# A hybrid decoder block on one core: start addresses of matmul operands in SBUF

## The chip, the cores and the metric

The kernel runs on one core of a Trainium2 chip. The metric is the device time of one execution in microseconds (us), as the median of three runs. SBUF is the on-chip memory; each of its 128 partitions holds a row of bytes, and a tile occupies the same bytes in every partition. An address below is the byte at which an operand starts in a partition, and "offset" is that address modulo 512.

## What is computed

One layer of a decoder: a normalization, one wide input projection, two token mixers side by side (gated linear attention, "GLA", and a sparse attention with compressed, selected and window branches, "NSA"), a gated merge with an output projection, and a SwiGLU channel mixer. 512 tokens, width 1024, SwiGLU width 2816, everything in float32.

```python
def reference(x, ...):
    h = rms_norm(x, norm_mix_pre[l])
    proj = h @ w_in[l]
    (...) = jnp.split(proj, split_points, axis=-1)
    o_gla = gla_mixer(g_q, g_k, g_v, g_r, g_a, ...)
    o_nsa = nsa_mixer(n_q, n_kc, n_vc, n_ks, n_vs, n_kw, n_vw, n_gate, ...)
    mixed = (jax.nn.sigmoid(merge_gla) * (o_gla @ w_proj_gla[l])
             + jax.nn.sigmoid(merge_nsa) * (o_nsa @ w_proj_nsa[l]))
    x = x + rms_norm(mixed @ w_out[l], norm_mix_post[l])
    h = rms_norm(x, norm_ffn_pre[l])
    f = (jax.nn.silu(h @ w_ffn_gate[l]) * (h @ w_ffn_up[l])) @ w_ffn_down[l]
    x = x + rms_norm(f, norm_ffn_post[l])
    return x
```

## The kernel before

Activations lie transposed, features on the partitions and tokens along them. A matmul multiplies 128x128 weights (stationary) with a moving operand of 128 rows and 512 tokens ("long") or 256 tokens ("short").

**Three matmuls for one.** Every float32 operand is split into a high part in the format fp32r and the low rest, and each product is three fp32r matmuls: high weights with high activations, high with low, low with high. The weights change with every matmul, so each matmul has a weight load of its own. `prod` (L199–211, matmuls L208 to L210) does this for long products.

**Seven products for eight.** The input projections of pairs of heads, the SwiGLU gate and up projections (but three plain columns) and most of the down projection are done by a scheme of Strassen's kind: two outputs by two halves of the tokens from seven short products, of sums of weights ("a11", "s2", "s3", "s1", "a22", "s4", "a12") with sums of activations ("b11", "t2", "t3", "t1", "t4", "b22", "b21"). A unit is such a set of seven: 7 x 12 = 84 matmuls of 256 tokens in the input units (`in_unit`, matmul L422) and the SwiGLU units (`unit`, matmul L1588), and 7 x 21 = 147 in the down products (`down_product`, L1900, four units, worked through in the order `seq`). Sums and splits of the weights for the next units are made meanwhile: raw weights arrive by DMA, DVE adds (L380 to L383 for the input, `sums_s` and `sums_t` for SwiGLU, `dsum` for down), ACT casts the high part, and the low part is a subtraction on DVE (L393, L1488) or a DMA that adds (L362, L1463).

**Stages in time.** The first normalization and the token-major projections (to 42 us), 12 input units (42 to 164), long input projections with GLA and the compressed branch, the attention among further projections (to about 410), projection and output (`out_half` L1315), plain SwiGLU columns (`ffn_half` L1386), SwiGLU units (`unit`, from 521), the rest of SwiGLU, long down products, the four down units (754 to 826) and the last normalization. Instructions are put in order per engine by the program; a tile's readers and writers wait for each other by semaphores.

**Weight buffers.** Long products take their weights from `Stream`, which fetches a raw tile and splits it into "whi" and "wlo", a pair of tiles with two buffers each. The units use the same two pairs as slots, with "s1", "s2", "s0", "uu", "d0", "d1", "hl2/hl3" and "g3" in turn (`slots`, `next_slot`, `w_slot`). Where each tile lies in SBUF follows from the pools and the order in which tiles are made.

Offsets of the operands as the program is built, with d = (weights − moving) modulo 512:

| products | moving, before | weights, before | moving, after | weights, after |
|---|---|---|---|---|
| input units | hT 480; t1 to t4 448 | s0 448; s1, s2, whi, wlo 480; uu 448 | 480 | 32; s0 64 |
| long products | hT 480; gla_hi 0, gla_lo 480; bh, bl 128 | whi, wlo 480 | 480 | 480 |
| last output products | hT 480 | rw 0; uu, d0, d1, we 32 | 480 | rw, we 480; uu, d0, d1 32 |
| plain SwiGLU columns | h2h, h2l 0 | whi, wlo 480; g3 64; uu, d1 and others 32 | 480 | 32; g3 64 |
| SwiGLU units | hT 480; x4, x6 0; x5 32 | whi, wlo 480; d0, d1, uu 32; hl 0; g3 64 | 480 | 32; g3 64 |
| down units | b11 64 and 0; t1 32; t2 0 and 32; t3 32 and 0; b21 0; hT 480 | whi, wlo 480; g3 64 | 480; t1, t2 32 | 32; a11 64; with t1, t2 96 |
| attention | 0 | 0 | 352 | 352 |

Counted over the program, of the 3688 short matmuls in fp32r after the change 3084 have d = 64, 444 have d = 96, 160 have d = 0. In the three stages that the prediction sums up these are 840 and 168 (input units), 1266 and 118 (the SwiGLU matmuls from 547 to 711 us, those that the trace of before pairs with the program), 504 and 84 (down).

Of the kernel before, what the change touches and what calls it, by code (L numbers as in the profile page):

```python
# [32 lines left out]

T_GQ, T_GK, T_NQ, T_KV, T_R, T_MA, T_MB = 0, 4, 8, 12, 16, 24, 32


class Stream:


    def __init__(self, nc, pool, ahead):  # L40
        self.nc, self.pool, self.ahead = nc, pool, ahead
        self.src, self.done, self.pos, self.made = [], {}, 0, 0
        self.on_dma, self.place, self.halved, self.low_pin = set(), {}, {}, {}
# [14 lines left out]
    def ahead_to(self, n):  # L58
        while self.made < min(n, len(self.src)):
# [54 lines left out]
def hybrid_block_kernel(ctx: ExitStack, tc: tile.TileContext, I, outT):  # L114
# [13 lines left out]
    one = base.tile([128, 1], F32, name="ones")  # L128
    ones = one.to_broadcast([128, 128])
    dve.memset(one, 1.0)  # L130
    mhalf = base.tile([128, 16], F32, name="mhalf")
    dve.memset(mhalf, -0.5)
    eps4 = base.tile([128, 1], F32, name="eps4")
    dve.memset(eps4, 4.0 * EPS)
    eps1 = base.tile([128, 1], F32, name="eps1")
# [7 lines left out]
    warm = base.tile([128, 1], F32, name="warm")  # L143
# [8 lines left out]
    b_alpha, g_gla = vecs[:, 32:36], vecs[:, 36:38]  # L152
    hT = base.tile([128, KD, S], F32R, name="hT_hi")
    hTl = base.tile([128, KD, S], F32R, name="hT_lo")
    rb_x = base.tile([128, S], F32, name="rb_x")
    rs_x = base.tile([128, NT], F32, name="rs_x")


    tk = Stream(nc, wts, 1)
# [12 lines left out]
    st = Stream(nc, wts, 1)  # L172
# [21 lines left out]
    sd = Stream(nc, wts, 1)  # L194
# [74 lines left out]
    tokb = mid.tile([128, NT, TOKW - 1024], F32, name="tokb")  # L269
# [10 lines left out]
    eld = tokv.tile([128, HG, 12], F32, name="eld")  # L280
    triu8 = tokv.tile([128, 128], U8, name="triu8")
# [4 lines left out]
    uu = [s1.tile([128, 1024], F32R, name="uu0")]  # L286
# [6 lines left out]
    tform.update({f: [tf.tile([128, 4, 256], F32R, name=f + x) for x in "hl"] for f in TF[1:]})  # L293
    uu.append(tf.tile([128, 1024], F32R, name="uu1"))
# [166 lines left out]
    def gates_low(tag):  # L461
        w_a2, keep = place("ksts", [16, 512], F32), place("kstw", [128, 8, 64], F32)
        aT, w3 = place("qst0", [80, S], F32R), place("qst1", [80, S], F32R)
        pool.dma_start(w_a2, I["w_alpha2"])
        make_keep(keep)
# [16 lines left out]
    def gates_in(hs, tag):  # L482
        for h in hs:
# [3 lines left out]
            low = us2[1] if h == 3 else place(("qst2", "qst3", "ksts")[h], [128, S], F32)  # L487
# [83 lines left out]
    for c in range(4):  # L571
# [6 lines left out]
        elif c == 2:  # L578
            first_pair()
# [1511 lines left out]
```

## Time and profile before

| | us |
|---|---|
| median of 3 runs | 838.19 (837.63 to 838.41) |
| the profiled execution, its own time | 837.62 |
| its span, first to last instruction | 835.8 |
| TensorE (PE) busy | 829.5 |
| VectorE (DVE) busy | 655.4 |
| ScalarE (ACT) busy | 525.8 |
| GpSimd (POOL) busy | 178.4 |

The profile is one execution. A row of a timeline has the start in us, a duration, the engine, the line, the operation and "output<-moving operand, weights", then the shapes and a count. Matmuls overlap in the pipeline, so a row's duration says little; the time from one start to the next is what a matmul costs. A row of the chain has the start, the duration of the piece, and "xN" where N instructions of one kind follow each other. A row of waits reads "engine tile line <- what ended the wait: us in total, times, longest".

### The profile page before, as it was taken

Reading aid. Unit: us, or ns where it says so; the run is one execution under the profiler, and the core shown is the slowest. Engines: PE = TensorE matmul, PEld = TensorE weight load, DVE = VectorE, ACT = ScalarE, POOL = GpSimd, SP = SyncE. Lnnn points to the kernel's source line nnn. Section 1 sums busy time; section 2 is a strip of 40 time slices with the busy share of each in tenths; the row PEclk is TensorE's granted clock in tenths of the full one; section 3 lists DMA queues with packets and bytes.
Section 4 is the critical chain, followed back from the end, with each engine's and each line's share of the span. In section 5 each row is a group of like instructions: output and inputs, shape, how many; then the busy total and the mean of one; then the engine's idle time right before and its main releaser. Section 6 shows DMA issues by size and latency. Waiting matters only on the chain.

```text
span 835.8 us, 14964 instructions
## 1 busy us (share of the span) xinstructions
PE 829.5 (99%) x5676; PEld 763.9 (91%) x5676; DVE 655.4 (78%) x1225; ACT 525.8 (63%) x953; POOL 178.4 (21%) x217
## 2 busy tenths in 40 slices
PE   9999999999999999999999999999999999999997
PEld 8999999988888888888878998999999999889996
DVE  7877989956678988877585388998777779739985
ACT  7765687646536878877445588576555667435543
POOL 0223222422321111111001355111111110001444
PEclk9999999999999999999999999999999999999999
DMA  7588788421233444444148759488777772325222
GB/s 256 143 220 185 172 178 184 91 76 50 84 130 92 98 114 121 107 110 105 39 126 327 198 150 235 113 224 205 194 195 184 188 160 65 106 83 177 89 102 102
DMA packets 45449, 120.75 MB, mean 144 GB/s; under 512 B 5981, under 2 KB 11373, under 8 KB 45249
## 3 DMA queue, kind: packets, MB, share of 16 engines
q1 hardware_dynamic: 30720, 82.62, 29.9%
q0 software_dynamic: 14080, 36.76, 24.7%
q8 instruction: 44, 0.72, 0.3%
q10 hardware_dynamic: 576, 0.41, 0.2%
q14 instruction: 29, 0.23, 0.1%
HBM read 105.10 MB, written 4.19 MB: 131 GB/s over the span
## 4 chain that ended last, share of the span: by engine, by line
PE 94%; DVE 3%; ACT 1%; DMA 0%; issue 0%; SPq 0%; DVEq 0%; ACTq 0%
PE ps_mm L208 6%; PE ps_mm L209 6%; PE ps_mm L210 6%; PE ps_mm L1588 6%; PE ps_sc L1588 5%; PE ps_tp L1588 5%; PE ps_acc L1588 5%; PE ps_sc L1900 4%; PE ps_mm L422 4%; PE ps_tp L422 4%; PE ps_acc L422 3%; PE ps_sc L422 3%; PE ps_tp L1137 2%; PE ps_acc L1900 2%; PE ps_mm L1900 2%; PE ps_sc L210 1%
## 5 line engine op out<-in xcount | busy, mean ns | idle before, releaser
L79 ACT CAST whi<-wraw 128x1024 fp32r<-128x1024 f32 (+3 forms) x56 | 54.2, 968 | 50.9 <-issue 13.3
L208 PE MATMUL ps_mm<-hT_hi,whi 128*128 128x512 f32 x152 | 61.8, 407 | 0.0
L86 DVE TENSOR_TENSOR wlo<-wraw,whi 128x1024 fp32r<-128x1024 f32 (+3 forms) x41 | 44.8, 1093 | 20.8 <-ACT whi L79 16.8
L210 PE MATMUL ps_mm<-hT_hi,wlo 128*128 128x512 f32 x152 | 60.0, 395 | 0.0
L209 PE MATMUL ps_mm<-hT_lo,whi 128*128 128x512 f32 x152 | 59.9, 394 | 0.0
L1096 ACT ACTIVATE p<-p,mx 128x512 f32<-128x512 f32 (+1 forms) x64 | 35.8, 559 | 9.2 <-DVE mx L1094 8.4
L226 DVE TENSOR_TENSOR pl<-ps_tp,ph 128x512 fp32r<-128x512 f32 (+1 forms) x64 | 31.2, 489 | 10.2 <-ACT ph L225 9.3
L1094 DVE CUSTOM_DVE_ANT_0 p<-ps_sc,causal 128x512 f32<-128x512 f32 (+1 forms) x64 | 30.0, 485 | 7.4 <-PE ps_sc L1087 7.2
L210 PEld LDWEIGHTS ps_mm<-hT_hi,wlo 128*128 128x128 f32 x152 | 28.6, 188 | 6.4 <-DVE wlo L86 0.3
L1463 POOL DMA_DIRECT2D w_uu<-in_w_up x19 | 16.8, 882 | 81.2 <-PE ps_mm L1588 20.9
L208 PEld LDWEIGHTS ps_mm<-hT_hi,whi 128*128 128x128 f32 x152 | 28.6, 188 | 5.5
L83 POOL DMA_DIRECT2D wlo<-wraw x15 | 13.2, 879 | 94.3 <-ACT wlo L82 93.8
L209 PEld LDWEIGHTS ps_mm<-hT_lo,whi 128*128 128x128 f32 x152 | 28.7, 189 | 4.4
L225 ACT CAST ph<-ps_tp 128x512 fp32r<-128x512 f32 (+1 forms) x64 | 26.4, 414 | 4.4 <-PE ps_tp L1137 3.7
L1137 PE MATMUL ps_tp<-ident,p 128*128 128x128 f32 x160 | 27.7, 272 | 0.0
L1137 PEld LDWEIGHTS ps_tp<-ident,p 128*128 128x128 f32 x160 | 20.8, 140 | 7.1
L208 PE MATMUL ps_mm<-gla_hi,whi 128*128 128x512 f32 x64 | 26.2, 409 | 0.0
L210 PE MATMUL ps_mm<-gla_hi,wlo 128*128 128x512 f32 x64 | 25.2, 394 | 0.0
L209 PE MATMUL ps_mm<-gla_lo,whi 128*128 128x512 f32 x64 | 25.2, 393 | 0.0
L1481 ACT CAST w_d1h<-s 128x1024 fp32r<-128x1024 f32 x13 | 13.6, 1050 | 16.2 <-issue 12.8
L1481 ACT CAST w_d0h<-s 128x1024 fp32r<-128x1024 f32 x12 | 12.6, 1050 | 17.2 <-issue 12.7
L1881 POOL TENSOR_TENSOR y<-y,us 128x256 f32<-128x256 f32 x6 | 6.8, 1155 | 71.8 <-DVE us L1878 71.8
(1270 smaller groups left out, 3436.1 us busy)
## 6 DMA issues: line engine op xcount, KB each, us to landing
wraw<-in_w_t SPq DMA_DIRECT2D x28, 512.0 KB, 3.6
wraw<-in_w_gate SPq DMA_DIRECT2D x21, 512.0 KB, 4.2
rw<-in_w_up SPq DMA_DIRECT2D x19, 512.0 KB, 4.7
wlo<-wraw POOLq DMA_DIRECT2D x15, 512.0 KB, 4.5
wlo<-in_w_gate POOLq DMA_DIRECT2D x13, 512.0 KB, 7.2
urw<-in_w_t SPq DMA_DIRECT2D x12, 512.0 KB, 5.7
w_uu<-in_w_up POOLq DMA_DIRECT2D x19, 256.0 KB, 4.1
raw<-in_w_down SPq DMA_DIRECT2D x10, 448.0 KB, 3.3
```

Of the source, the lines that this page charges most:

```text
L79: self.cast = self.nc.scalar.copy(hi[:, :cols], raw[:, :cols])
L86: self.nc.vector.tensor_tensor(out=lo[:, :cols], in0=raw[:, :cols], in1=hi[:, :cols].bitcast(F32), op=OP.subtract)
L208: pe.matmul(ps[:, t], wh[:, c], xh(k)[:, t], start=(k == 0), stop=False)
L209: pe.matmul(ps[:, t], wh[:, c], xl(k)[:, t], start=False, stop=False)
L210: marks.append(pe.matmul(ps[:, t], wl[:, c], xh(k)[:, t], start=False, stop=(k == ktot - 1)))
L226: return dve.tensor_tensor(out=lo, in0=src, in1=hi.bitcast(F32), op=OP.subtract)
L422: pe.matmul(o, w[:, c], x_of(b, q, low), start=(first and q == 0 and i == 0), stop=(q == 3 and i == 2), skip_group_check=True)
L1094: dve.tensor_tensor_reduce(out=o, in0=s, in1=causal[:, S - n:S], scale=-1.0, scalar=-NEG, op0=OP.add, op1=OP.min, accum_out=mx[:, i:i + 1])
L1096: act.activation(out=o, in_=o, func=AF.Exp, scale=-1.0, bias=mx[:, i:i + 1], accum_out=z[:, i:i + 1])
L1137: queued["turn"] = pe.transpose(tp[:, i * 128:(i + 1) * 128], p[:, OFF[i] + k * 128:OFF[i] + (k + 1) * 128], ident)
L1588: pe.matmul(o, w[:, c], x[q], start=(first and q == 0 and i == 0), stop=(q == 3 and i == 2), skip_group_check=True)
L1900: pe.matmul(o, w[:, c], x[q], start=(first and q == 0 and i == 0), stop=(q == KH - 1 and i == 2), skip_group_check=True)
```

## The change

All of SBUF is laid out so that nearly every moving operand starts at offset 480. The weights of short products start at 32 (some at 64, and 96 in the down products whose moving operand is at 32), those of long products at 480.

- "whi" and "wlo" with their two buffers become four regions of one tile "wbuf" (class `Regions`): `pair(i, shift)` gives a high and a low region of 1024 columns, shifted by 16 elements (64 bytes) for short products and by `D_SHIFT` in the down products. The regions are taken in turn as the buffers were.
- Small pads ("off2" to "off5") and a "room" tile per tag set where the tiles of a pool begin. "hl2/hl3" become one tile "hlc". The forms t1 to t3 of the down products exchange their tags.
- Four one-column constants become columns of one tile. The factor `keep` of the GLA scan becomes a tile of bytes of its own (it lay in two shared tiles, was made twice, and held float32). With that `gates_minus(3)` is issued one step of the loop over `j` earlier.
- The triangular mask is loaded at the start into "rb_x" and cast by GpSimd; before, it was loaded after the input units and cast by DVE.

The sequence of matmuls stays the same but for eight rows at the end of the attention. At the start of GpSimd's program stood ("rs_x" is the first normalization's factor per token, "ident" the identity for transposes, "s0l" the low part of the first unit's weights):

```order
masks.py:197 MEMSET ident 128x128
masks.py:199 ISA
masks.py:199 AFFINE_SELECT ident<-ident 128x128
L242 TENSOR_TENSOR rs_x<-rs_x,mhalf 128x4
L362 DMA s0l<-in_w_t 128x512 x2
```

Now stands there:

```order
masks.py:197 MEMSET ident 128x128
L170 DMA rb_x<-in_triu 128x128
masks.py:199 ISA
masks.py:199 AFFINE_SELECT ident<-ident 128x128
L171 CAST triu_86<-rb_x 128x128
L259 TENSOR_TENSOR rs_x<-rs_x,consts 128x4
L383 DMA s0l<-in_w_t 128x512 x2
```

The mask's load and cast are new there, and the factor's power comes behind the cast.

On DVE, at the end of the input units, stood ("us" and "merge" are sums of the unit's products from PSUM, "ps_"; "lam" is the scan of GLA, "e_" its factors, "eld" a small table of them):

```order
L447 TENSOR_TENSOR ksts<-ksts,rb_x 128x512
L498 TENSOR_TENSOR lam_161<-low,lam_161 128x512
L658 TENSOR_TENSOR eld<-eld 128x4
L664 TENSOR_TENSOR e_uu_1977<-gq_149,e_ssum 128x4x64
L665 TENSOR_TENSOR e_uu_1977<-gq_149,e_ssum 128x4x64
L426 TENSOR_TENSOR us<-ps_acc,us 128x256
L666 TENSOR_TENSOR e_t2h<-gk_153,e_ssum 128x4x64
L658 TENSOR_TENSOR eld<-eld 128x4
L426 TENSOR_TENSOR us<-ps_tp,us 128x256
L683 CAST triu_164<-e_uu_1977 128x128
L664 TENSOR_TENSOR e_uu_1977<-gq_149,e_ssum 128x4x64
L426 TENSOR_TENSOR merge<-ps_tp,us 128x256
```

Now stands there (the small table is a part of "tokb"):

```order
L468 TENSOR_TENSOR ksts<-ksts,rb_x 128x512
L675 TENSOR_TENSOR tokb<-tokb 128x4 x2
L447 TENSOR_TENSOR us<-ps_acc,us 128x256
L683 TENSOR_TENSOR e_t2h<-gk_148,e_ssum 128x4x64
L447 TENSOR_TENSOR us<-ps_tp,us 128x256
L681 TENSOR_TENSOR e_t3h<-gq_144,e_ssum 128x4x64 x2
L682 TENSOR_TENSOR e_t3h<-gq_144,e_ssum 128x4x64
L447 TENSOR_TENSOR merge<-ps_tp,us 128x256
```

The subtraction for "lam" (L498) has moved ahead and the mask's cast (L683) is gone; the GLA factors have moved behind the second sum from PSUM.

The diff, cut to what is spoken of:

```diff
+class Regions:
+    def __init__(self, pool, first):
+        self.buf, self.turn = pool.tile([128, 4 * 1024 + 128], F32R, name="wbuf"), first
+    def pair(self, i, shift):
+        at = 2048 * (i % 2) + shift
+        return self.buf[:, at:at + 1024], self.buf[:, at + 1024:at + 2048]
+    def next(self, shift=0):
+        self.turn += 1
+        return self.pair(self.turn - 1, shift)
...
-                hi = self.pool.tile([128, 1024], F32R, tag="whi", bufs=2, name="whi")
-                lo = self.pool.tile([128, 1024], F32R, tag="wlo", bufs=2, name="wlo")
+                hi, lo = self.regions.next(SHIFT if key in self.shifted else 0)
...
+    pool.dma_start(rb_x[:, 0:128], I["triu"])
+    pool.tensor_copy(triu8, rb_x[:, 0:128])
...
+    st.shifted = {("g", 0), ("u", 0)}
...
+    tform["t3"] = [t3h, tf.tile([128, 4, 256], F32R, name="t3l")]
+    tform.update({f: [tf.tile([128, 4, 256], F32R, name=f + x) for x in "hl"] for f in TF[2:]})
+    tf.tile([128, 16], F32, name="off2")
+    uu = [tf.tile([128, 1024], F32R, name="uu%d" % i) for i in range(2)]
+    tf.tile([128, 8], F32, name="off3")
     sform0 = [tf.tile([128, 1024], F32R, name="s0" + x) for x in "hl"]
...
-        slots.extend([wts.tile([128, 1024], F32R, tag="w" + x, bufs=2, name="w" + x) for x in ("hi", "lo")]
-                     for _ in range(2))
+        slots.extend(regions.pair(i, SHIFT) for i in range(2))
...
-        elif j in (7, 8, 9, 10):
+        elif j in (7, 8, 9):
             with tc.issue_after(queued["s1"].ins):
                 gates_minus(j - 7)
                 if j < 9:
                     gates_scan(j - 7)
-            if j == 10:
-                make_keep(us2[1].rearrange("p (c t) -> p c t", t=64))
+                else:
+                    gates_minus(3)
...
-    pool.dma_start(ec[:, 0:128], I["triu"])
-    with tc.issue_after(queued["s3"].ins):
-        dve.tensor_copy(triu8, ec[:, 0:128])
...
+    def w_slot(which, shift=SHIFT):
         if which == "w":
-            return (wts.tile([128, 1024], F32R, tag="whi", bufs=2, name="whi"),
-                    wts.tile([128, 1024], F32R, tag="wlo", bufs=2, name="wlo"))
+            return regions.next(shift)
+        if which == "c":
+            t = hlc(F32R, "w_hl")
+            return [t[:, c:c + 1024] for c in (SHIFT, 1024 + SHIFT)]
...
+    D_SHIFT = {"w": (24, 32, 16), "g3": (0, 8, 120)}
...
-        hi, lo = [x[:, :KW] for x in w_slot(("w", "g3", "w")[j % 3])]
+        which = ("w", "g3", "w")[j % 3]
+        shift = D_SHIFT[which][0 if a == "a11" else 1 if b in ("t1", "t2") else 2]
+        hi, lo = [x[:, shift:shift + KW] for x in w_slot(which, 0)]
```

More of the change, by code (lines that the diff above doesn't have):

```diff
@@ L127, in hybrid_block_kernel @@
     make_identity(nc, ident)
-    one = base.tile([128, 1], F32, name="ones")
+    cst = base.tile([128, 8], F32, name="consts")
+    one, eps1, warm, mhalf = cst[:, 0:1], cst[:, 1:2], cst[:, 2:3], cst[:, 4:8]
     ones = one.to_broadcast([128, 128])
     dve.memset(one, 1.0)
-    mhalf = base.tile([128, 16], F32, name="mhalf")
     dve.memset(mhalf, -0.5)
-    eps4 = base.tile([128, 1], F32, name="eps4")
-    dve.memset(eps4, 4.0 * EPS)
-    eps1 = base.tile([128, 1], F32, name="eps1")
     dve.memset(eps1, EPS)
@@ L152, in hybrid_block_kernel @@
     b_alpha, g_gla = vecs[:, 32:36], vecs[:, 36:38]
+    rs_x = base.tile([128, NT], F32, name="rs_x")
+    triu8 = base.tile([128, 128], U8, name="triu8")
     hT = base.tile([128, KD, S], F32R, name="hT_hi")
@@ L155, in hybrid_block_kernel @@
     rb_x = base.tile([128, S], F32, name="rb_x")
-    rs_x = base.tile([128, NT], F32, name="rs_x")
-    tk = Stream(nc, wts, 1)
+    pool.dma_start(rb_x[:, 0:128], I["triu"])
+    pool.tensor_copy(triu8, rb_x[:, 0:128])
+    regions = Regions(wts, 1)
+    tk = Stream(nc, wts, 1, regions)
     for c in range(4):
@@ L170, in hybrid_block_kernel @@
     tk.halved[("tok", 0, 0)] = TG
-    st = Stream(nc, wts, 1)
+    st = Stream(nc, wts, 1, regions)
     for c in range(4):
@@ L268, in hybrid_block_kernel @@
     ah = {}
-    tokb = mid.tile([128, NT, TOKW - 1024], F32, name="tokb")
+    room = mid.tile([128, 1280], F32, name="tokb")
+    NB = NT * (TOKW - 1024)
+    tokb, eld = [room[:, a:b].rearrange("p (i c) -> p i c", i=4) for a, b in ((0, NB), (NB, NB + 12 * HG))]
     C_VS, C_VW, C_GATE, C_A = 0, 128, 256, 280
@@ L579, in hybrid_block_kernel @@
             first_pair()
+    regions.turn += 1
     with tc.issue_after(x_rb.ins), tc.issue_after(rs_made.ins):
@@ L673, in gla_factors @@
         gst[h] = [q4, kx, ku, dec]
-    ea, eb, ec, ed = [early(tag) for tag in ("ssum", "urw0", "uu0", "t2h")]
+    ea, eb, ec, ed = [early(tag) for tag in ("ssum", "urw0", "t3h", "t2h")]
     e1, e2 = cols(ea, 0, S), cols(ea, S, NT, 2, 64)
@@ L1279, in flat, with hlc, wtile @@
         return t.rearrange("p a t -> p (a t)")
+    def hlc(dtype, name):
+        return ffn.tile([128, 2048 + SHIFT], dtype, tag="hlc", name=name)
+    def wtile(tag):
+        return flat(ffn.tile([128, 2, S], F32R, tag=tag, bufs=2 if tag in ("uu", "rw") else 1, name="w_" + tag))
+    for tag in [x + str(i) for x in ("a", "e", "hh") for i in range(4)] + ["hl0", "hl1"]:
+        quad(tag, F32, "room")
+    acc = ffn.tile([128, S], F32, name="acc1")
+    for tag, shape in (("sl", [128, S]), ("rw", [128, 2, S]), ("us", [128, 2, 256]), ("sa", [128, 2, S]),
+                       ("wk", [128, 3, 256])):
+        for _ in range(2):
+            ffn.tile(shape, F32, tag=tag, bufs=2, name="room")
+    hlc(F32, "room")
+    for tag in ("uu", "uu", "d0h", "d0l", "d1h", "d1l"):
+        wtile(tag)
+    ffn.tile([128, 8], F32, name="off5")
+    for tag in ("g3h", "g3l"):
+        wtile(tag)
     xs = quads("xs", 4, F32, "a")
@@ L1301, in hybrid_block_kernel @@
         st.place[key] = lambda: [flat(quad("e%d" % i, F32R, "we%d" % i)) for i in (2, 3)]
-    h2h, h2l = quads("h2h", 4, F32R, "hh"), quads("h2l", 4, F32R, "hl")
+    h2h, h2l = quads("h2h", 4, F32R, "hh"), quads("h2l", 2, F32R, "hl")
+    h2l23 = hlc(F32R, "h2l23")[:, 0:2048].rearrange("p (b a t) -> p b a t", b=2, a=2)
+    h2l += [h2l23[:, i] for i in range(2)]
     x1 = [slot(k) for k in range(8)]
-    acc = ffn.tile([128, S], F32, name="acc1")
     def square_into(ps, n):
```

42 lines of the change are left out of this document (16 added, 26 removed).

## The prediction

> **What bounds the kernel now.** First the page: the shares of the engines, the granted clock and the chain of work that ended last.
>
> ```profile
> span 835.8 us, 14964 instructions
> PE 829.5 (99%) x5676; PEld 763.9 (91%) x5676; DVE 655.4 (78%) x1225; ACT 525.8 (63%) x953; POOL 178.4 (21%) x217
> PEclk9999999999999999999999999999999999999999
> PE 94%; DVE 3%; ACT 1%; DMA 0%; issue 0%; SPq 0%; DVEq 0%; ACTq 0%
> ```
>
> The chain is TensorE's for 94% of the span, at full clock throughout, and there are as many weight loads (PEld) as matmuls: every matmul brings its own 128x128 weights, read while the matmul before it streams. Next the waits of TensorE, all that are long enough to be listed, and one of GpSimd that is needed below:
>
> ```profile
> PE ps_acc L149 <- DVE eps L136: 0.9, 1, 0.9
> PE ps_sc L1588 <- ACT us L1605: 0.5, 1, 0.5
> PE ps_mm L1588 <- DVE w_hl L1488: 0.4, 1, 0.4
> POOL rs_x L242 <- DVE rs_x L241: 22.7, 1, 22.7
> ```
>
> TensorE waits 1.8 us for others in 835.8. So the kernel is as long as its matmuls are apart, and a change of addresses can act in one way only: on the time from the start of one matmul to the start of the next. The timeline of TensorE shows that this is not one number. All rows here are 128x128 by 128x256 matmuls in the same number format, one behind the other, with no wait between them: stretches of the output halves, of a SwiGLU unit (twice), and the last product of the input stage from the chain.
>
> ```profile
> 458.05 0.28 PE L209 MATMUL ps_sc<-hT_lo,w_uu 128*128 128x256 f32 x1
> ...
> 468.25 0.28 PE L209 MATMUL ps_acc<-hT_lo,we 128*128 128x256 f32 x1
> ```
>
> ```profile
> 613.38 0.28 PE L1588 MATMUL ps_sc<-hT_hi,w_d0h 128*128 128x256 f32 x1
> ...
> 617.62 0.28 PE L1588 MATMUL ps_sc<-x5h,w_uu 128*128 128x256 f32 x1
> ```
>
> ```profile
> 591.98 0.28 PE L1588 MATMUL ps_acc<-hT_hi,w_g3h 128*128 128x256 f32 x1
> ...
> 593.39 0.28 PE L1588 MATMUL ps_acc<-hT_hi,w_hl 128*128 128x256 f32 x1
> ```
>
> ```profile
> 162.46 1.44 PE ps_acc L422 x12
> ```
>
> In order: 90 matmuls from 458.05 to 468.25 (113.3 ns each), 36 from 613.38 to 617.62 (117.8), 12 from 591.98 to 593.39 (117.5), 12 in 1.44 us (120.0). What tells them apart is where their operands start in a partition of SBUF, modulo 512 bytes; I take d = (start of the next weights − start of the moving operand) modulo 512. The last has both at 480, d=0. The third has 480 against 64, d=96. The first two are the same class, 480 against 32, d=64: this class has two steady states, a short one of 113.3 and a long one of 117.8, and stays in the one it is in for dozens of matmuls, across products. I call them the short and the long lock.
>
> **The change part by part.** The orders of the engines are as before but for a dozen rows on DVE, GpSimd and the last of the attention, so the edits are these.
>
> *Short products (256 wide).* Every moving operand goes to 480 and most weights to 32, so 2610 matmuls of the three long stages get d=64; s0, g3 and the down products' a11 get d=96 (370). By stage:
>
> Input units, 12 units of 84 matmuls; the chain from the first:
>
> ```profile
> 42.53 2.81 PE ps_sc L422 x24
> ...
> 62.46 2.86 PE ps_sc L422 x24
> ```
>
> From 42.53 to 62.46 are two units, 168 matmuls in 19.93 us, 118.6 ns each. After: 140 at d=64 and 28 at d=96. In the short lock 140 x 113.3 + 28 x 117.5 = 19.15 us, 0.78 less, and six times that is 4.7 us. In the long lock 19.78 us, six times 0.15 = 0.9 us.
>
> SwiGLU units, from 547 to 711; from the chain the first and the last of four whose stretches are whole there:
>
> ```profile
> 572.29 9.94 PE ps_sc L1588 x84
> ...
> 622.02 9.82 PE ps_mm L1588 x84
> ```
>
> These are 168 in 19.76 us, 117.6 ns, which I take for the stage. After: 1266 at d=64, 118 at d=96. Short: 1266 x (117.6 − 113.3) = 5.4 us. Long: 1266 x 0.2 = 0.2 us lost.
>
> Down products, 28 of 21 matmuls:
>
> ```profile
> 754.61 17.37 PE ps_sc L1900 x147
> 771.98 17.33 PE ps_mm L1900 x147
> ```
>
> This is 294 in 34.70 us, 118.0 ns. After: 504 at d=64, 84 at d=96. Short: 504 x 4.7 + 84 x 0.5 = 2.4 us. Long: 0.1 us.
>
> Output halves and plain SwiGLU products, 440 to 547: half of them already have d=64 and are short, as the first stretch above. The weights of the last output product (we) move from d=64 to d=0: 48 x (120.0 − 113.3) = 0.3 us lost. The plain ones move from d=0 and d=64 to d=64 and 96; by the same spacings the whole is between −0.5 (long) and +0.6 us (short), and I take +0.3.
>
> *Long products (512 wide).* One steady stretch with moving operand and weights at 480, and the second half of the projection, whose moving operand (bh, bl) is at 128:
>
> ```profile
> 228.19 0.39 PE L208 MATMUL ps_mm<-hT_hi,whi 128*128 128x512 f32 x1
> ...
> 232.95 0.39 PE L208 MATMUL ps_mm<-hT_hi,whi 128*128 128x512 f32 x1
> ```
>
> ```profile
> 416.72 0.40 PE L209 MATMUL ps_sc<-bl,whi 128*128 128x512 f32 x1
> ...
> 438.04 0.40 PE L210 MATMUL ps_sc<-bh,wlo 128*128 128x512 f32 x1
> ```
>
> 21 in 4.76 us are 226.7 ns each; 91 in 21.32 us are 234.3. So d=0, the worst for short products, is the best here, and bh and bl move to it: 96 x 7.6 = 0.7 us. The rest (gla, moved from 0 to 480) lies partly beside the chains of the attention; of its possible 0.6 I take 0.3. Together 1.0 us, and no less than 0.7 unless the stretch has another cause.
>
> *Start.* The triangular mask (64 KB) is now fetched among the first loads, before it was fetched and cast later.
>
> ```profile
> GB/s 256 143 220 185 172 178 184 91 76 50 84 130 92 98 114 121 107 110 105 39 126 327 198 150 235 113 224 205 194 195 184 188 160 65 106 83 177 89 102 102
> ```
>
> At the 256 GB/s of the first slice its bytes cost 0.26 us if the loads bound the start, nothing if not: 0.2. The cast that waits for it now stands on GpSimd ahead of the power for rs_x, which waits 22.7 us for DVE today (row above): that hides it. DVE loses the cast, two memsets and a subtraction moved by one step; TensorE waits for none of it. Without that cover each is under a microsecond, once. The regions of the one weight tile are taken in turn as the buffers were, and what waits for a buffer waits for the same matmuls.
>
> *Which lock.* This decides between 13.6 us in all (4.7 + 5.4 + 2.4 + 0.3 + 1.0 − 0.2) and 1.1 us (0.9 − 0.2 + 0.1 − 0.5 + 1.0 − 0.2). The trace shows entries into d=64:
>
> ```profile
> 526.55 0.28 PE L1588 MATMUL ps_tp<-hT_hi,w_d0l 128*128 128x256 f32 x1
> ...
> 527.57 0.28 PE L1588 MATMUL ps_tp<-hT_hi,w_d0l 128*128 128x256 f32 x1
> ```
>
> ```profile
> 478.36 0.28 PE L210 MATMUL ps_mm<-hT_hi,w_d1l 128*128 128x256 f32 x1
> ...
> 480.83 0.28 PE L210 MATMUL ps_mm<-hT_hi,w_d1l 128*128 128x256 f32 x1
> ```
>
> The first follows three matmuls at d=96 and is short (9 in 1.02 us, 113.3). The second follows a pause and is long (21 in 2.47, 117.6). The long stretch at 613 follows matmuls at d=0, both operands at 480, and so do the other long ones of the SwiGLU units that I looked at. In the changed kernel d=0 is gone from the three long stages; entries come from d=96 or from pauses. I read seven of those kinds in this trace, three after d=96 and four after pauses, and the one at 478 is the only long one. So I put six sevenths of the 12.5 us between the two ends in the short lock: 13.6 − 12.5/7 = 11.8 us.
>
> The profiled execution took 837.62 us, span 835.8 and 1.8 around it; the median of the three runs is 838.19. With 11.8 less the profiled one is at 825.8 and the median at 826.4, and that is the forecast.
>
> **The rivals.** *The long lock nearly everywhere*: 1.1 us less, 837.1. For it: the stretch at 613 and the one at 478. Against: what led into it at 613 is gone. Chance 0.07.
>
> *Addresses do nothing*, and the spacings above come from what else the program does at those places: then only the 0.2 us of the start stays, 838.4. Against it stands one shape at 113.3, 117.5, 117.8 and 120.0 with a clock of 9 in every slice and no wait. Chance 0.05. The Trainium skill holds with this rival: "TensorE: Matmul & The Clock Gate", section "Step-by-step: what each phase is for", gives the array two independent SBUF read ports, one for the moving operand and one for the weights, by which their addresses could not matter to each other; the 113.3 to 120.0 ns of this trace speak against it.
>
> *The preparation of the weights becomes the bound.* DVE makes the weight sums of each unit.
>
> ```profile
> 42.40:163.60 121.20, 121.20 (x1016) 120.81 (x1015) 105.20 (x175) 83.58 (x141) 35.00 (x44) 1.00 0.76 171
> ```
>
> The columns are us, then busy us of PE, PEld, DVE, ACT and POOL, clock, DMA share and GB/s. DVE is busy 105.2 of 121.2 us. The short lock makes this stage 116.5, DVE 90% busy, still with room on average; but a sum that comes in time today by less than 0.4 us per unit would be waited for. If the input units lose all that they win (six sevenths of the way from 0.9 to 4.7, 4.2 us), the time is 830.6; if the SwiGLU units lose half of theirs as well, 832.9. For it: the wait for w_hl that is there already. Chance 0.14.
>
> *A slower third state*, the other side: with all of the moving operands at 480, the d=64 products settle where the d=0 ones do, at 120.0. Units 840 x 1.4 = 1.2, SwiGLU 1266 x 2.4 = 3.0, down 504 x 2.0 = 1.0, the plain ones 0.6, less the 0.8 of the other edits: 5.0 slower, 843.2. It decides from a mean spacing of about 118.3 ns over the 2610 matmuls (118.0 now, and 0.8 us in 2610 is 0.3 ns). Against it: no stretch at d=64 holds above 117.8. Chance 0.05.
>
> **How the numbers follow.** Forecast 0.66 (six sevenths short, with all cases from three fifths to all short, 824.6 to 830), and 0.03 for mixes above that. The range goes from 823.5 (all short, nothing lost at the start, 0.2, the plain products and the gla products at their best, 0.3 each, and 0.3 for the spread of the runs) to 833.5, past the rival of the weights; left out are the long lock, no effect and the slower state, 0.17. A measurement here can tell 0.2%, 1.7 us, from no change. Faster by more than that: forecast, mixes and the weights, 0.83. Within it: the long lock and no effect, 0.12. Slower: 0.05.
>
> **What would show it.** In the changed trace the chain's runs of 84 matmuls in the SwiGLU units should read 9.55 us where short and 9.9 where long, two input units 19.2 us against 19.93, 147 down matmuls 16.7 us against 17.35, the projection's second half 227 ns. The waits of TensorE should stay under 3 us in all. I am wrong if 9.9 prevails, if the shape shows spacings other than 113, 117.5 and 120, or if waits for the weight sums on DVE come up between 42 and 164 us.

## The result and the profile after

The changed kernel takes 832.44 us (median of 4 runs, 832.12 to 832.59) against 838.30 (4 runs, 837.63 to 838.72) beside it: ratio 0.993, with a 95% interval of 0.9913 to 0.9948. It is 5.9 us faster, half of the 11.8 that were forecast. The profiled execution took 832.12 us.

The page of the changed kernel, then all waits of TensorE that are long enough to be listed:

```profile
span 830.3 us, 14965 instructions
PE 822.6 (99%) x5676; PEld 757.6 (91%) x5676; DVE 653.4 (79%) x1223; ACT 525.7 (63%) x953; POOL 180.0 (22%) x216
PE 92%; DVE 4%; ACT 1%; issue 1%; DMA 1%; SPq 0%; DVEq 0%; ACTq 0%
```

```profile
PE ps_acc L161 <- DVE consts L149: 0.9, 1, 0.9
PE ps_sc L1622 <- DVE us L1626: 0.6, 1, 0.6
PE ps_mm L339 <- ACT hT_hi L279: 0.4, 1, 0.4
PE ps_mm L1622 <- DVE w_hl L1522: 0.4, 1, 0.4
PE ps_mm L443 <- DVE us L447: 0.3, 1, 0.3
PE ps_sc L1016 <- DVE kdg L992: 0.2, 1, 0.2
```

The same instructions, and 2.8 us of waits: still a kernel as long as its matmuls are apart. The chain of the changed kernel, at the places where that of before was shown (start, duration, what; from the start of the first input unit to the start of the third, with the one product at d=96 of the first, 12 matmuls in 1.44 us; then two SwiGLU units and two down units):

```profile
43.32 2.78 PE ps_sc L443 x24
...
51.55 1.44 PE ps_sc L443 x12
...
62.51 2.81 PE ps_sc L443 x24
...
599.34 9.85 PE ps_tp L1622 x84
609.18 9.69 PE ps_sc L1622 x84
...
750.19 16.98 PE ps_sc L1936 x147
767.17 17.03 PE ps_mm L1936 x147
```

The two input units went from 19.93 to 19.19 us (43.32 to 62.51), where 19.15 was the figure for the short lock. The SwiGLU units take 9.85 and 9.69, between the 9.55 of the short lock and the 9.9 of the long one, and 147 down matmuls 17.0 where 16.7 was short. Two more stretches of TensorE's timeline, the projection's second half (from its first matmul to the 97th start) and a stretch of the output halves (from the first to the 73rd):

```profile
413.41 0.39 PE L225 MATMUL ps_sc<-bh,wbuf 128*128 128x512 f32 x1
...
435.17 0.39 PE L225 MATMUL ps_mm<-hT_hi,wbuf 128*128 128x512 f32 x1
...
454.62 0.28 PE L225 MATMUL ps_sc<-hT_hi,w_uu 128*128 128x256 f32 x1
...
463.10 0.28 PE L225 MATMUL ps_acc<-hT_hi,we 128*128 128x256 f32 x1
```

The long products of the projection came to 226.7 ns as forecast (96 in 21.76 us). The products with w_uu, w_d0 and w_d1, which stood in the short lock before, are in the long one now (72 in 8.48 us, 117.8 ns), though their d is 64 in both kernels.

By stage, from the same matmul to the same matmul in both traces; the forecast of a term is six sevenths of the way between its two ends:

| stage | before, us | after, us | change | forecast |
|---|---|---|---|---|
| start to the first input unit | 39.58 | 40.37 | +0.8 | +0.2 |
| input units | 121.37 | 118.17 | −3.2 | −4.2 |
| stages of long products (GLA, attention, projection, long down) | | | −0.6 | −1.0 |
| output halves, plain columns, first SwiGLU units | | | +0.6 | −0.2 |
| SwiGLU units | 163.36 | 161.39 | −2.0 | −4.6 |
| down units | 71.50 | 70.19 | −1.3 | −2.1 |
| end | | | +0.2 | 0 |

To read the locks over whole stages, I sorted the 256-wide matmuls at d=64 of the profiled execution by the mean spacing of the seven starts around each. Short are 665 of 833 in the input units (105 long, the rest between), 671 of 1253 in the SwiGLU units (507 long), 278 of 485 in the down units (171 long): 63% short in the three stages, where six sevenths, 86%, were put. The output halves have 23 short of 143 (135 of 188 before). The products at d=96 are 119.7 ns apart in the input units and 119.0 in the other two, where 117.5 was put.

What happens where a lock changes? A timeline from the changed kernel, 629.71 to 631.4 in a SwiGLU unit: ScalarE's rows around its copy of the first product's sum, and TensorE's as it comes to the third product (weights w_hl).

```profile
629.71 1.05 ACT L1495 ACTIVATE w_g3l<-wraw 128x1024 fp32r<-128x1024 f32 x1
...
630.66 0.36 ACT L1639 COPY us<-ps_acc 128x256 f32<-128x256 f32 x1
...
631.01 0.28 PE L1622 MATMUL ps_acc<-hT_hi,w_d1l 128*128 128x256 f32 x1
...
631.13 0.33 PE L1622 MATMUL ps_acc<-hT_hi,w_hl 128*128 128x256 f32 x1
...
631.29 0.28 PE L1622 MATMUL ps_acc<-hT_lo,w_hl 128*128 128x256 f32 x1
...
631.41 0.40 PE L1622 MATMUL ps_acc<-hT_hi,w_hl 128*128 128x256 f32 x2
```

The first product has its sum in one half of a PSUM bank, the third goes to the other half of the same bank and waits for the copy. The copy stood behind a 1.05-us cast on ScalarE and ended at 631.02, as the third product was due: its first matmul is 0.05 us longer than the rest, the next start comes after 166 ns, and from there the spacing is 118 where it was 113 up to 631.01. The SwiGLU stage has 15 such stops now (over 135 ns from start to start; 1.0 us in all over the usual spacing), 3 before (0.2 us); the input units 5 (0.9 us, one alone 0.6), 3 before (0.3).

Not every stop changes the lock. The long stretches of this stage's trace begin at 545, 592, 602, 631 and 670, each behind a stop (the first behind one at 544.9, just ahead of the stage), and together they hold nearly all of its long matmuls; behind the stops at 573, 582 and 661, and behind those from 692 on, TensorE goes on in the short lock. Most of the long stretches end at a product at d=96; the one from 602 ends at 613.3 between two products at d=64, with no stop.

### The profile page after: what moved, and what is told of

Read it like the earlier page. It is cut to its first block, busy times and chain, and to the rows that moved or that the text cites. A ratio compares the mean times of both kernels' runs of the same rounds, so it can differ in the third digit from the quotient of the medians.

```text
span 830.3 us, 14965 instructions
## 1 busy us (share of the span) xinstructions
PE 822.6 (99%) x5676; PEld 757.6 (91%) x5676; DVE 653.4 (79%) x1223; ACT 525.7 (63%) x953; POOL 180.0 (22%) x216
## 4 chain that ended last, share of the span: by engine, by line
PE 92%; DVE 4%; ACT 1%; issue 1%; DMA 1%; SPq 0%; DVEq 0%; ACTq 0%
PE ps_mm L225 7%; PE ps_mm L226 6%; PE ps_mm L227 6%; PE ps_mm L1622 6%; PE ps_sc L1622 5%; PE ps_tp L1622 5%; PE ps_acc L1622 5%; PE ps_sc L1936 4%; PE ps_mm L443 4%; PE ps_tp L443 3%; PE ps_acc L443 3%; PE ps_sc L443 3%; PE ps_tp L1151 2%; PE ps_acc L1936 2%; PE ps_mm L1936 2%; PE ps_sc L226 1%
## 5 line engine op out<-in xcount | busy, mean ns | idle before, releaser
L95 ACT CAST wbuf<-wraw 128x1024 fp32r<-128x1024 f32 (+3 forms) x56 | 54.2, 968 | 47.7 <-issue 13.3
L102 DVE TENSOR_TENSOR wbuf<-wraw,wbuf 128x1024 fp32r<-128x1024 f32 (+3 forms) x41 | 44.4, 1084 | 22.7 <-ACT wbuf L95 18.6
L225 PE MATMUL ps_mm<-hT_hi,wbuf 128*128 128x512 f32 x152 | 61.8, 407 | 0.0
L226 PE MATMUL ps_mm<-hT_lo,wbuf 128*128 128x512 f32 x152 | 60.0, 395 | 0.0
L227 PE MATMUL ps_mm<-hT_hi,wbuf 128*128 128x512 f32 x152 | 59.8, 393 | 0.0
L227 PEld LDWEIGHTS ps_mm<-hT_hi,wbuf 128*128 128x128 f32 x152 | 28.5, 188 | 6.5 <-DVE wbuf L102 0.4
L225 PEld LDWEIGHTS ps_mm<-hT_hi,wbuf 128*128 128x128 f32 x152 | 28.6, 188 | 5.5
L99 POOL DMA_DIRECT2D wbuf<-wraw x15 | 13.1, 870 | 94.5 <-ACT wbuf L98 94.5
L226 PEld LDWEIGHTS ps_mm<-hT_lo,wbuf 128*128 128x128 f32 x152 | 28.7, 189 | 4.5
L225 PE MATMUL ps_mm<-gla_hi,wbuf 128*128 128x512 f32 x64 | 26.0, 407 | 0.0
L226 PE MATMUL ps_mm<-gla_lo,wbuf 128*128 128x512 f32 x64 | 25.2, 394 | 0.0
L227 PE MATMUL ps_mm<-gla_hi,wbuf 128*128 128x512 f32 x64 | 25.1, 393 | 0.0
```

What stands on the lines that cost most here:

```text
L95: self.cast = self.nc.scalar.copy(hi[:, :cols], raw[:, :cols])
L102: self.nc.vector.tensor_tensor(out=lo[:, :cols], in0=raw[:, :cols], in1=hi[:, :cols].bitcast(F32), op=OP.subtract)
L225: pe.matmul(ps[:, t], wh[:, c], xh(k)[:, t], start=(k == 0), stop=False)
L226: pe.matmul(ps[:, t], wh[:, c], xl(k)[:, t], start=False, stop=False)
L227: marks.append(pe.matmul(ps[:, t], wl[:, c], xh(k)[:, t], start=False, stop=(k == ktot - 1)))
```

## The experiments

Three questions were open. What keeps 30% of the products in the long lock: the stops alone, so that the d=96 products between the others are dear and nothing else; or do the d=96 products bear on the lock too, and in which direction? The main theory is that of the stops: a lock is lost where TensorE comes to a bank too early, and without that the short lock holds. Does d alone set the spacing, or the place in the program? And does the mask's early load cost the 0.8 us of the start? Each ratio is to the kernel before on the same chip, with its 95% interval.

**e1: no d=96.** Pads moved, so that s0, g3 and the down products' a11 have d=64 too:

```diff
-    tf.tile([128, 8], F32, name="off3")
     sform0 = [tf.tile([128, 1024], F32R, name="s0" + x) for x in "hl"]
+    tf.tile([128, 8], F32, name="off3")
...
-    D_SHIFT = {"w": (24, 32, 16), "g3": (0, 8, 120)}
+    D_SHIFT = {"w": (16, 32, 16), "g3": (0, 16, 0)}
```

> The 444 short matmuls that stand at d=96 (weights s0, g3 and the down products' a11 at offset 64) get d=64 like the others (those weights at 32). In the changed kernel they take 119.3 ns on the mean, locked at 120.0 where the product before was in the short lock. Theory P (a pause of TensorE throws it into the long lock, nothing else does; d=96 only costs its own time): the 444 go to between 113.3 and 117.8 as their neighbours, mean 115.1, 444 x 4.2 = 1.9 us less, 830.5 us, and the share of the long lock among d=64 stays near 40% in the SwiGLU stage. Rival R (a product at d=96 puts TensorE back into the short lock, and without it a long lock lasts until the next pause): the long share in the input units and the SwiGLU stage rises to 60% or more, which costs 2610 x 0.25 x 4.5 = 2.9 us against the 1.9 won: 833 us or slower.

Measured: 833.28 us, 0.9941 [0.9929, 0.9954], no faster than the change itself, although the matmuls at d=96, of which I could place 366 in the changed trace, lost their 119 to 120 ns. Its chain:

```profile
609.22 9.89 PE ps_sc L1622 x84
619.11 9.89 PE ps_mm L1622 x84
```

9.89 us for 84 is 117.7: whole units in the long lock. In the SwiGLU units 1065 of 1379 are long now, in the input units 524 of 998. So d=96 is dear by itself, but it is also what ends a long lock; without it a lock that is entered stays. That only pauses and stops decide falls.

**e2: no wait for the copy.** ScalarE's copy reads another tile, so the third product has nothing to wait for on ScalarE (the SwiGLU sums lack their first product):

```diff
-        act.copy(us[:, 0, :], r1)
+        act.copy(us[:, 0, :], rb_x[:, h0])
```

> In the SwiGLU units the copy by ACT of the first product's result out of PSUM reads another tile of the same size instead (the sum is left without that product), so the third product, which writes the same PSUM bank, has no copy to wait for; ACT has the same work. Theory P (TensorE in the short lock comes up to that copy, stands still for 0.1 us and often goes on in the long lock): of the 15 pauses between 545 and 709 us at most 5 stay, the long share of the stage falls from 40% to 20% or less, and the stage becomes 0.7 us (pauses) and 1253 x 0.2 x 4.5 = 1.1 us shorter: about 830.6 us. Rival W (the weights that DVE prepares are what TensorE overtakes, and the copy is only the last of several): other pauses take their place and the time stays at 832.4 within 0.4.

Measured: 833.22 us, 0.9937 [0.9924, 0.9951]. Not one stop is left at the third product, but the fourth now meets its own: DVE's sum of the second product, which shares the other bank. The chain of this kernel passes through it:

```profile
599.75 6.82 PE ps_tp L1622 x60
...
613.04 0.34 DVE us L1626
613.38 0.04 issue
613.42 5.73 PE ps_sc L1622 x48
```

The stage has 18 stops (1.9 us) and 446 long of 1250. One wait took the place of another; this alone tells nothing about the theory of the stops. The stage took 161.89 us here. In e3 and e6 below, whose SwiGLU units are those of the changed kernel, it took 161.81 and 161.67, against 161.39 in the changed kernel itself: the share of the long lock differs by so much from one execution to the next.

**e4: a map.** A kernel with matmuls alone: sections of 48 at each d (moving operand at 480), a pause behind each, then sections that go from one d to another, then 24 of 512 columns at each d. Its matmuls:

```diff
...
+            w = at(W, (mo + d) % 512, q + (8 if i == 2 else 0), 128)
+            m = at(M, mo, 2 * (q % 2) * (n // 256) + (12 if i == 1 else 0), n)
+            pe.matmul(ps[:, 0:n], w, m, start=(first and k == 0), stop=(last and k == count - 1), skip_group_check=True)
...
```

> None of the block is computed: runs of matmuls at chosen offsets with the weights changing each time, no other engine at work but for a copy out of PSUM between runs (the pause). Moving operand at 480 with d from 0 to 480 in steps of 32 (48 each), at 0, 32 and 352 in steps of 64, 20 runs at d=64 after pauses of different lengths, runs that go from d=96, d=0 and d=64 to d=64 and d=96, and 512-wide matmuls at all d. If the offsets alone set the spacing: d=64 shows 113.3 or 117.8 and nothing else, d=0 120.0, d=96 117.4 after a pause and 120.0 after the short lock, the same at each moving offset; after pauses of 20 lengths both locks come up, after d=0 the long one, after d=96 the short one. If the spacing came from the other engines' work: one spacing for all.

Its timeline: the sections at d=64, 96 and 256; 12 at d=0 followed by 36 at d=64; 12 at d=96 (after a pause) followed by 36 at d=64; then the 512-wide ones at d=64 and 256.

```profile
20.32 5.73 PE L67 MATMUL ps<-mv,wt 128*128 128x256 f32 x48 [0.58 <-DVE ps L76]
26.63 5.96 PE L67 MATMUL ps<-mv,wt 128*128 128x256 f32 x48 [0.58 <-DVE ps L76]
...
59.05 6.02 PE L67 MATMUL ps<-mv,wt 128*128 128x256 f32 x48 [0.58 <-DVE ps L76]
...
318.58 5.94 PE L67 MATMUL ps<-mv,wt 128*128 128x256 f32 x48 [0.58 <-DVE ps L76]
...
333.14 5.76 PE L67 MATMUL ps<-mv,wt 128*128 128x256 f32 x48 [0.86 <-DVE ps L76]
...
408.63 5.87 PE L67 MATMUL ps<-mv,wt 128*128 128x512 f32 x24 [0.58 <-DVE ps L76]
...
447.22 5.73 PE L67 MATMUL ps<-mv,wt 128*128 128x512 f32 x24 [0.58 <-DVE ps L76]
```

Mean spacings of the later half of each section, in ns, for 256 columns:

| d | 0 | 32 | 64 | 96 | 128 | 160 | 192 | 224 |
|---|---|---|---|---|---|---|---|---|
| spacing | 120.0 | 118.3 | 113.3 | 118.6 | 118.6 | 120.0 | 113.3 | 116.7 |

From 256 on it repeats within 0.1, but for two: 224 + 256 = 480 gives 117.8, and 192 + 256 = 448 gives 117.8 in place of 113.3, as does 192 with the moving operand at 0, 32 or 352. So d=192 has two locks like d=64. For 512 columns d=0 and 256 have 226.7, 192 and 448 have 228.8, the rest 232.8 to 234.6. No other engine works beside these matmuls, so d sets the spacing: that addresses do nothing is excluded. The Trainium skill, "TensorE: Matmul & The Clock Gate", section "Step-by-step: what each phase is for", gives the array two independent SBUF read ports, one for the moving operand and one for the weight loads; read as saying that the two addresses cannot matter to each other, this does not hold for these matmuls, by the 113.3 to 120.0 ns of the table. All 28 sections that start at d=64 after a pause are short, where both locks had been expected. Behind d=0 the products at d=64 are long (4 of 4), behind d=96 that was itself entered from the short lock they are short (4 of 4; the d=96 ones are 120.0 there), behind d=96 after a pause short in 3 of 4.

**e5: own banks.** In twelve SwiGLU units, 571 to 690 us, each of the four sums has a bank of its own, as in the input units, two banks more per unit than before:

```diff
-        p1, p2 = bank(tag), bank(tag)
-        r1, rb, r2, ra = p1[:, 0:256], p1[:, 256:512], p2[:, 0:256], p2[:, 256:512]
+        own = N0 + 5 <= n < 20
+        if own:
+            tags = (("sc", "mm"), ("acc", "tp"))[(n - N0 - 5) % 2]
+            r1, r2, rb, ra = [bank(tag)[:, 0:256] for tag in tags for _ in range(2)]
...
```

> Twelve of the SwiGLU units (those from the sixth on) get a PSUM bank of their own for each of their four sums, as the input units have, in place of two sums in a bank: the third product waits no longer for ACT's copy of the first, nor the fourth for DVE's sum of the second. The weights' offsets are those of the changed kernel. Theory P' (TensorE in the short lock overtakes the clearing of the banks, first ACT's copy, and where that is gone DVE's sum; each such stop costs 0.1 us and may leave it in the long lock): the stops between 570 and 690 us go, the long share of the stage falls from 40% to under 25%, the stage (161.4 us in the changed kernel) to 159.5, the whole to 830.5. Rival W (the preparation of weights is next behind): stops come up at other places and the stage stays above 161.

Measured: 830.57 us, 0.9904 [0.9891, 0.9918]. Its chain, where a unit is 24 + 48 + 12:

```profile
572.25 5.44 PE ps_mm L1627 x48
577.69 1.36 PE ps_sc L1627 x12
579.05 2.72 PE ps_acc L1627 x24
581.77 5.44 PE ps_tp L1627 x48
```

Four rows at 113.3 ns (48 in 5.44). From 570 to 690 there is no stop; 1168 of 1260 in the stage are short and 22 long, and the stage takes 158.81 us, 2.6 less than in the changed kernel: all that its term had lost to the forecast. The theory of the stops holds for this stage. "PSUM — Partial Sum Buffer" in the Trainium skill, section "PSUM bank collisions raise a hardware error", wants PSUM guarded by bank (strictly, by bank and group of partitions), not by address: by that rule the two halves of a bank wait for each other's readers, and the stops of the changed kernel, gone here with the sharing, agree.

**e11: own banks in the kernel before**, the same edit without the change of addresses.

> The kernel before, its addresses as they were, with PSUM banks of their own for the twelve SwiGLU units. Theory P' (the stops at the banks come up only because the short lock makes a product 1.36 us instead of 1.41): nothing to gain here, one stop at 594 us less, 838.2 us within 0.4. Rival (the banks held TensorE up before the change too, and give 1.9 us by themselves): 836.3. Its start is that of the kernel before: the second half of the first token weights is cast at 4.9 us there and at 5.5 to 6.6 in all the kernels with the new layout so far; if the start only scatters, it may be late here too.

Measured: 838.16 us (11 runs) against 838.39 (15 runs), 0.9998 [0.9989, 1.0007]: nothing. One row of busy time shows the four cases, from 545 to 700 us (us, busy us of PE with its matmuls in brackets, then PEld, DVE, ACT, POOL): before, before with own banks, the changed kernel, the changed kernel with own banks.

```profile
545.00:700.00 155.00, 154.59 (x1311) 154.17 (x1310) 124.89 (x221) 94.64 (x140) 25.93 (x30) 1.00 0.77 185
```

```profile
545.00:700.00 155.00, 154.59 (x1312) 154.24 (x1312) 125.15 (x221) 95.05 (x141) 25.98 (x30) 1.00 0.78 186
```

```profile
545.00:700.00 155.00, 155.00 (x1333) 154.78 (x1334) 126.61 (x224) 96.80 (x146) 25.25 (x30) 1.00 0.76 181
```

```profile
545.00:700.00 155.00, 155.00 (x1357) 154.89 (x1357) 128.86 (x230) 99.30 (x152) 25.15 (x30) 1.00 0.77 183
```

The shared banks cost nothing as long as products are slow (one more matmul in 155 us), and 24 matmuls once they are fast.

**e7: what leads where.** Matmuls alone again: 24 at d=64, then k at another d ("X"), then 24 at d=64, once from the short lock and once from the long one; then 64 sections of 24 at d=64, each let go by DVE after a slightly longer wait, the last 32 with copies on ScalarE and a DMA beside them.

```diff
+    for x in (32, 96, 128, 160, 192, 224, 0):
+        for k in (3, 12):
+            section([(480, 64, 24, 256), (480, x, k, 256), (480, 64, 24, 256)])
+            section([(480, 0, 12, 256), (480, 64, 24, 256), (480, x, k, 256), (480, 64, 24, 256)])
...
```

> Runs of 256-wide matmuls alone, moving operand at 480. First: 24 at d=64, then 3 or 12 at another d, then 24 at d=64, once from the short lock (after a pause), once from the long one (after 12 at d=0). Theory R (which lock follows is set by the step before, the same each time): d=96 keeps the short lock and ends the long one with 12 and perhaps with 3; some other d does it too. If a lock lasts through a few matmuls at another d, the long entry stays long with 3. Then 2 x 32 runs of 24 at d=64 that wait a little for DVE, longer from run to run by 8 ns, the second 32 with copies on ACT and a stream of DMA beside: if the length of the wait decides the lock, long and short alternate with the length in both halves; if the other engines' traffic throws matmuls into the long lock, only the second half shows it.

With k=12, the last 24 are short from either lock behind d=96, 128, 160, 192 and 224; they are long from either behind d=0; behind d=32 they keep the lock that was there. With k=3 less is sure: the short lock is lost behind d=128, 160 and 0, and the long one stays behind d=32, 160 and 0; one section began in the long lock though it followed a pause. Two rows from the timeline, from the short lock through 12 at d=96 and through 12 at d=192:

```profile
54.35 7.17 PE L67 MATMUL ps<-mv,wt 128*128 128x256 f32 x60 [0.58 <-DVE ps L76]
...
150.15 7.08 PE L67 MATMUL ps<-mv,wt 128*128 128x256 f32 x60 [0.58 <-DVE ps L76]
```

The second is 0.09 us shorter: 12 times about 7 ns. Entered from the short lock, d=192 stays at 113.3 where d=96 takes 120.0, and it leads back as well. Of the 32 sections without other work 5 ended long, of those with copies and a DMA 14. Not all of them are restarts: 21 and 18 begin behind a pause (over 135 ns from start to start), and of these 3 and 10 ended long. Pauses of nearly the same length led to either lock (358 ns to the short one, 360 to the long one, both in the second half), so the length alone does not decide; whether the work of the other engines bears on it, and what does decide, was not found.

**e9: d=192 in place of 96.** s0, g3 and a11 at 160 (their d 192), s1 and s2 of the input units at 288 (d=320, like 64 in the map):

```diff
-    tf.tile([128, 8], F32, name="off3")
+    tf.tile([128, 32], F32, name="off3")
...
+        s2.tile([128, 40], F32, name="off6")
...
-    D_SHIFT = {"w": (24, 32, 16), "g3": (0, 8, 120)}
+    D_SHIFT = {"w": (48, 32, 16), "g3": (0, 112, 96)}
```

> As the changed kernel, but the 444 matmuls at d=96 stand at d=192 (weights s0, g3 and the down products' a11 at offset 160; s1 and s2 go to 288, which is d=320). By the two maps the spacing repeats with d every 256, so d=320 counts as d=64, d=192 has the two locks 113.3 and 117.8 as well, keeps the short one, and a step from d=192 back to d=64 ends in the short lock from either. Expected by that: 444 x (119.3 - 113.5) = 2.6 us less, the share of the long lock at d=64 as it is (12% in the input units, 40% in the SwiGLU stage), 829.8 us. If the reset needs the 12 slow matmuls at d=96, the share rises as in the run without d=96 and the time stays at 832 or above.

**e8: both**, the edits of e5 and e9.

> PSUM banks of their own for twelve SwiGLU units and d=192 in place of d=96 together. If the two causes are separate their gains add: 830.6 - 2.5 = 828.1 us; SwiGLU stage 158.0 us (158.8 with the banks alone), input units 117.3 (118.2), down 69.8 (70.2). If faster products only bring up the next wait (weights, sums on DVE), less than half of it: above 829.4.

Measured: e9 831.81 us, 0.9921 [0.9907, 0.9936]; e8 828.72 us, 0.9883 [0.9868, 0.9897]. Alone, the cheaper products bring TensorE into more stops (22 of 1.7 us in the SwiGLU units, 9 of 1.2 in the input units) and win little over the change, 2 us short of what was expected. With own banks (e8) whole units are short. This one has no product of g3, so its row is that of e5:

```profile
600.65 5.44 PE ps_tp L1628 x48
606.09 1.36 PE ps_acc L1628 x12
607.45 2.72 PE ps_sc L1628 x24
```

84 in 9.52 us, the 9.55 that the prediction named, and 158.16 us for the stage.

**e10: d=192 for more of the down products**, e8 with s3 and s1 of the down units at d=192 as well:

```diff
...
-        shift = D_SHIFT[which][0 if a == "a11" else 1 if b in ("t1", "t2") else 2]
+        shift = D_SHIFT[which][0 if a in ("a11", "s3") else 1 if b == "t2" else 3 if b == "t1" else 2]
```

> As the run with both, and in the down products the third and fourth (s3 with t3, s1 with t1) get their weights at d=192. In the changed kernel these two are in the long lock in nearly every unit: the step of the moving operand from 32 to 480 and back shifts the phase (t2 short, t3 long, t1 long, a22 short). If the lock is set by the step of addresses, d=192 changes which lock follows: from all short, 8 products x 21 x 4.5 = 0.8 us less than the run with both, to no gain if the long lock moves to the next product.

Measured: 829.04 us, 0.9887 [0.9870, 0.9903]; the down units take 70.60 us, 70.29 in e8. The products at d=192 are 117.4 ns apart there: they were entered from the long lock and stayed in theirs. No gain. In e9 and e8 the s2 products, which follow most of the a11 now at d=192, are long in all four units (117.8), where three of four were short in the changed kernel. So what e7 shows, with the moving operand at one address throughout, does not carry over to the down units, where it steps from 480 to 32 and back.

**e3, e6: the mask later.** e3 ties the load to the last piece of the first split; e6 puts it on SyncE's queue behind x:

```diff
-    pool.dma_start(rb_x[:, 0:128], I["triu"])
-    pool.tensor_copy(triu8, rb_x[:, 0:128])
...
+    nc.sync.dma_start(rb_x[:, 0:128], I["triu"])
+    pool.tensor_copy(triu8, rb_x[:, 0:128])
```

> The load of the triangular mask and its cast are put behind the loads of x (the load is issued when the last split of x is done); all else as in the changed kernel. The first input unit starts at 43.16 us in the changed kernel, 42.37 before. If the 64 KB among the first loads are the cause of the 0.79 us: 42.4 again, and 831.7 us in all. If the cause is another (the single weight tile, the constants): 43.1 and 832.4.

> The mask's load goes to SyncE's queue behind the eight loads of x, its cast stays on GpSimd (in the run before, the load was still issued at 1.3 us, since that edit ordered it after nothing that GpSimd had to wait for). If the mask among the first loads is the cause of the later start: first input unit at 42.4 to 42.6 us, 0.5 us less than the changed kernel. If the start only scatters from run to run (42.6 to 43.4 us in the kernels so far with the same first instructions): no difference in the median beyond 0.3 us.

Measured: e3 832.87 us, 0.9937 [0.9924, 0.9949], but the load was still issued at 1.3 us, so this run tells nothing of the mask; e6 832.17 us, 0.9930 [0.9917, 0.9944], start 40.04 us. Over all profiles the start is 39.58 (before), 40.37 (after), 39.82 (e1), 40.59, 40.29, 40.12, 40.04, 40.44, 40.60, 40.46, 40.50 (e12), and 40.36 in e11, whose first instructions are those of before. It follows ScalarE's cast of the second half of the first weights (4.89 us in before, 6.27 after), which waits for its DMA. The rows of before and of e11:

```profile
4.89 0.56 ACT L73 CAST whi<-wraw 128x440 fp32r<-128x440 f32 x1 [0.58 <-DMA wraw<-in_w_tok]
```

```profile
6.29 0.56 ACT L73 CAST whi<-wraw 128x440 fp32r<-128x440 f32 x1 [1.88 <-DMA wraw<-in_w_tok]
```

So the first loads scatter by over a microsecond from one execution to the next, and the 0.8 us cannot be put down to the mask.

**e12: the best of these**, e8 with the mask on SyncE as in e6.

> As the run with both (banks and d=192), with the mask's load on SyncE's queue behind the loads of x. By the run with that edit alone 0.3 us less or nothing: 828.4 to 828.7 us. If the mask among the first loads is the cause of the late start, the first unit starts by 42.8 us instead of 43.2.

Measured: 828.31 us (828.26 to 828.53), 0.9881 [0.9868, 0.9895]. It beats both kernels, the change by about 4 us; from e8 it can't be told apart.

## Why the prediction was half right

**Right.** What bounds the kernel, and that the addresses act through the spacing: the map repeats 113.3, 117.8 and 120.0 with nothing else running. The two locks at d=64 and their sizes. The sign and most of the long products (−0.6 us; the projection's 226.7 ns to the digit; gla's 0.3 did not show). No product at d=64 settled at 120: the slower third state fell.

**Wrong: the step "Which lock".** It took six of seven entries in the trace of before as the share of time in the short lock. The trace after showed 63% in the three stages, and 2.4 us of the loss stand there. Two things were found that this count could not see; the first is shown for the SwiGLU units, the second lies outside the three stages, and why 0.6 us were lost in the down units stays open.
- *The short lock makes its own way out.* A product of 12 takes 1.36 us in it and 1.41 in the long one. Those 0.05 us a product bring the third and fourth products of a SwiGLU unit to a bank before ScalarE or DVE has cleared its other half. The stop costs under 0.1 us; the long lock behind it costs 4.5 ns a matmul until something ends it. The slower kernel in which the entries were read had 3 of these stops in the stage, not 15. e5 removed them, won 2.6 us and brought the stage to its forecast; e11 shows that there was nothing to win before.
- *Rows that moved to d=0 were not followed by what stands behind them.* The prediction itself said that the long stretches follow d=0, and cleared the three long stages of it. But rw moved from d=32 to d=0 in the output halves, and behind it w_uu, w_d0 and w_d1 went from short to long. With the plain columns and the first units that is the loss of 0.6 us where a gain of 0.2 stood. That d=0 leads to long was seen in e4 and e7 each time; that rw is the cause here was not tried by itself.

**Mis-sized: d=96 at 117.5.** Entered from the short lock it takes 119 to 120; the row at 117.5 in the trace of before stood behind products at d=480. Over 366 matmuls that is about 0.7 us. Its other effect, to end a long lock, had no price in the prediction; e1, no faster without these products, shows that it is worth at least about as much as they cost.

Together, from the rows of the changed kernel: against the mean of 113.9 that the step put, d=64 costs 1.7 us more in the SwiGLU units (1253 x 1.34), 0.6 in the down units (485 x 1.25) and 0.1 in the input units; d=96 0.7; more and longer stops 1.4; output halves, plain columns and first units 0.8; long products 0.4; start and end 0.8. That is 6.5 for the 6.3 us that are missing between the profiled executions.

**The rival of the weights' preparation** named this time (832.9), and it was for its sake that the range reached beyond 830; but it did not name the cause, so that the time lies in the range is in part luck. No new wait for weights came up (the 0.4 us for w_hl stood there before); TensorE did overtake the other engines, but at the clearing of PSUM banks, not at the weights. The one stop of 0.6 us in the input units is of that kind too (`ps_mm L443 <- DVE us L447`): the fifth product takes up the third's bank before DVE has read it.

Open: what picks the lock at a restart; why the down products with t3 and t1 (s3, s1) are long in nearly every unit; why a long lock can end with no stop and no other d, as at 613.3.

## What to carry to other kernels

Where every matmul brings its own weights, the spacing of the matmuls is a thing to measure: run the shape alone over the possible offsets between weights and moving operand before laying out SBUF, 256 and 512 columns each by itself, since the best offset of one was the worst of the other. When a kernel gets faster by a few per cent per product, look for the readers that had just kept up, above all those that share a PSUM bank with the next product, and free them in the same step: here the banks alone were worth nothing, the addresses alone 5.9 us, and both, with the dear offset replaced, 10. When a state has memory, follow each edited product to the ones behind it; a share counted in the old trace does not carry over.

## What the runs showed of the hardware

- The spacing of fp32r matmuls with a weight load each depends on the start of the weights less the start of the moving operand, with a period of 256 bytes: 113.3 to 120.0 ns for 256 columns, 226.7 to 234.6 for 512 (e4; 224 and 480 differ, 116.7 and 117.8).
- At d=64 and 192 there are two steady states, 113.3 and 117.8, that mostly last until a pause or another d. With the moving operand at one address, 12 matmuls at d=96, 128, 160, 192 or 224 led to the short one and 12 at d=0 to the long one (e7; in e4 one of eight runs behind d=96 was long).
- A stop of 0.05 us can change the state (the timeline at 631), and need not (573, 661).
- The first loads of a kernel scatter: one cast waited 0.58 us for its DMA in before and 1.88 in e11, with the same instructions.
